# PSUM accumulators of a hybrid attention and recurrence layer: one pool of two banks, or a pool for each stage

## The chip, the cores and the metric

The kernel runs on one core of a Trainium2 chip. The metric is the device time of one execution in microseconds (us); the kernel before took 1431.96 us (median of three runs, 1424.61 to 1434.63). The engines are PE (TensorE, matrix products), DVE (VectorE), ACT (ScalarE), POOL (GpSimd) and SP (which issues the DMAs). A matrix product is written by PE into PSUM, a memory of eight banks, each of 512 fp32 numbers for each of 128 partitions, and is read from there by DVE or ACT, which is called its evacuation. A bank can take the next product only when its evacuation has ended.

## The reference

One decoder layer on 1024 tokens of width 1024, in fp32:

```
h   = rmsnorm(x);  p = h @ W_in          # q,k,v of 3 head groups, gates, recurrence inputs, merge gates
A   = dilated sliding-window attention   # 3 groups x 8 heads of 64, (window, dilation) = (128,1), (512,4), (2048,16),
                                         # merged per head by the softmax denominators
B   = RWKV-7 recurrence                  # 8 heads of 64
yA  = (A * silu(zA)) @ W_up_attn;  yB = (B * silu(zB)) @ W_up_rwkv
out = (sigmoid(ga) * yA + sigmoid(gb) * yB) @ W_out
x   = x + rmsnorm(out)
```

## The kernel before, in words

Every large product is made of three fp32r products: activations and weights are split in a high and a low part (`whi` by DVE or ACT, L135 and L137, `wlo` by POOL, L138), and hi x hi, lo x hi and hi x lo are summed in one PSUM bank, a tile named `acc`. A projection (`proj_steps`) has for each 128 columns of W_in two halves of 512 tokens, and each half is a group of 24 matmuls into one `acc` tile, which `evac` then reads.

The program has three stages.

- The recurrence, from the start to about 565 us of the span. Its order on PE is written out by hand (the tables PROLOGUE and LOOP), with projections filled in between. It uses all eight banks: two for `acc`, six in four pools of its own (`ps_ch`, `ps_y`, `ps_g`, `ps_i`).
- The attention, about 565 to 1155 us: four head pairs of about 150 us, each with three groups g = 0, 1, 2. For a group come the projections of q (evacuated by ACT L852 and DVE L853 for each of two heads), k (ACT L860, DVE L862), and v (DVE L888). The scores of a head are eight small products into tiles `pw` (L874, L875), each read at once by DVE (L876), which adds the bias and leaves a row maximum in `st`; `nm` (L879) is its negative, and ACT takes eight exponentials (L882). Tiles `pw` also take the transposes of v (L893, read by ACT L896 and DVE L897), of the weights (L949, read by ACT L952 as `ph` and DVE L953 as `pl`) and of `st` (L977). The products with v go to tiles `pv` (L961, L963), read into `num` by ACT L970 and DVE L971. After the third group of a pair, `group_weights` sends the maxima and sums through DRAM (tiles `mt`, `md`, `gs`; DVE L979, L980, then L998 to L1009).
- The last part, to the end: the remaining gate projections (evacuated by DVE L467), the two up-projections (L788 to L790, evacuated by DVE L1057 and L1073), and the product with W_out (L1102 to L1104), whose weights are loaded and split during the up-projection of the attention.

The pool `accp` of two banks (L224) is open for the whole program. In the attention `ps_w` (L804) has four banks and `ps_pv` two; in the last part only the two `acc` banks are used, and six stand empty. Beyond the recurrence the order of instructions on each engine is chosen by the framework's scheduler, which simulates a timeline and takes the instructions roughly in program order. The order is fixed before the program runs; an engine whose next instruction must wait holds up all that stand behind it.

Of the kernel before, what the change touches and what calls it, by code (L numbers as in the profile page):

```python
# [14 lines left out]
PSUM = bass.MemoryType.PSUM  # L15
# [97 lines left out]
class Kernel:  # L113
# [103 lines left out]
    def start(self):  # L217
        nc, tc, ctx, a = self.nc, self.tc, self.ctx, self.a
        pool = lambda **k: ctx.enter_context(tc.tile_pool(**k))
        self.cst = cst = pool(name="cst", bufs=1)  # L220
        self.wst = pool(name="wst", bufs=3)
        self.whl = pool(name="whl", bufs=3)
        self.ev = pool(name="ev", bufs=2)
        self.acc = pool(name="accp", bufs=2, space=PSUM)  # L224
        self.dram = pool(name="dram", bufs=1, space=DRAM)
        self.hstack = ExitStack()
        self.hpool = self.hstack.enter_context(tc.tile_pool(name="hT", bufs=1, side="right"))
        self.w_in = a["w_in"][0]
        self.sstack = ExitStack()
        self.small = self.sstack.enter_context(tc.tile_pool(name="small", bufs=1))  # L230

        self.ident = cst.tile([P, P], F32, name="ident")
        make_identity(nc, self.ident)
        self.eps = cst.tile([P, 3], F32, name="eps")
        nc.vector.memset(self.eps[:, 0:1], RMS_EPS)
        nc.vector.memset(self.eps[:, 1:2], GN_EPS)
        nc.vector.memset(self.eps[:, 2:3], 0.0)
        self.gain = cst.tile([P, KT], F32, name="gain")
        warm = cst.tile([P, 1], F32, name="warm")
        nc.scalar.activation(warm, self.eps[:, 2:3], AF.Sqrt)  # L240

        self.hT = []
        xr = a["x"][0].rearrange("(i r) d -> r i d", r=16)
        with tc.tile_pool(name="xin", bufs=1) as xin, tc.tile_pool(name="xps", bufs=4, space=PSUM) as xps:
            tiles = []

            def load(t):
                x = xin.tile([P, D], F32, name="x", tag="x", bufs=5)
                nc.sync.dma_start(x[0:64], xr[2 * t])
                nc.sync.dma_start(x[64:128], xr[2 * t + 1])  # L250
                tiles.append(x)

            for t in range(4):
                load(t)
            nc.sync.dma_start(self.gain, a["pre_norm_gain"].rearrange("o (k p) -> p (o k)", p=P))
            self.small_loads()
            for half in range(2):
                hh = self.hpool.tile([P, KT, 512], F32R, name=f"hh{half}")
                hl = self.hpool.tile([P, KT, 512], F32R, name=f"hl{half}")
                self.hT.append((hh, hl))  # L260
                if half:
                    self.w_wa = self.load_split(self.w_in, KT, OFF_WA)
                xs = []
                for j in range(4):
                    if half:
                        load(4 + j)
                    x = tiles[half * 4 + j]
                    sq = xin.tile([P, D], F32, name="sq", tag="sq", bufs=2)
                    st = xin.tile([P, 2], F32, name="st", tag="st", bufs=4)
                    if half:  # L270
                        nc.vector.tensor_tensor_reduce(sq, x, x, 1.0, 0.0, ALU.mult, ALU.add, st[:, 0:1])
                    else:
                        nc.scalar.activation(sq, x, AF.Square, accum_out=st[:, 0:1])
                    nc.scalar.activation(st[:, 1:2], st[:, 0:1], AF.Sqrt, bias=self.eps[:, 0:1], scale=1.0 / D)
                    nc.vector.reciprocal(st[:, 0:1], st[:, 1:2])
                    xn = xin.tile([P, D], F32, name="xn", tag="xn", bufs=5)
                    nc.vector.tensor_scalar(xn, x, st[:, 0:1], None, ALU.mult)
                    xs.append(xn)
                for k in range(KT):
                    ps = xps.tile([P, 512], F32, name="xT", tag="xT")  # L280
                    for j in range(4):
                        nc.tensor.transpose(ps[:, j * P:(j + 1) * P], xs[j][:, k * P:(k + 1) * P], self.ident)
                    nc.scalar.activation(hh[:, k], ps, AF.Copy, scale=self.gain[:, k:k + 1])
                    nc.vector.scalar_tensor_tensor(hl[:, k], ps, self.gain[:, k:k + 1], hh[:, k].bitcast(F32),
                                                   ALU.mult, ALU.subtract)
# [61 lines left out]
    def rwkv(self):  # L347
# [5 lines left out]
        with ExitStack() as ctx:  # L353
            pool = lambda **k: ctx.enter_context(tc.tile_pool(**k))
# [3 lines left out]
            self.ps_y = pool(name="ps_y", bufs=1, space=PSUM)  # L358
            self.ps_g = pool(name="ps_g", bufs=2, space=PSUM)
            self.ps_i = pool(name="ps_i", bufs=1, space=PSUM)  # L360

            self.sgn = rc.tile([P, 1], F32, name="sgn")
            nc.vector.memset(self.sgn[0:C], -1.0)
# [430 lines left out]
    def attention(self):  # L794
        nc, tc, a, cst = self.nc, self.tc, self.a, self.cst
        self.oat_d = self.dram.tile([NPAIR, P, S], F32, name="oat_d")
        self.n_md = 0
        self.hi_on_dve = True
        with ExitStack() as ctx:
            pool = lambda **k: ctx.enter_context(tc.tile_pool(**k))  # L800
            self.at = at = pool(name="at", bufs=1, side="right")
            early = ExitStack()
            self.ae = ae = early.enter_context(tc.tile_pool(name="ae", bufs=1))
            self.ps_w = pool(name="ps_w", bufs=4, space=PSUM)  # L804
            self.ps_pv = pool(name="ps_pv", bufs=2, space=PSUM)
            self.bias = []
            for i in range(2):
                b = ae.tile([P, 640], F32, name=f"bias{i}")
                nc.vector.memset(b[:, 512:], NEG)
                self.bias.append(b)  # L810

            self.kl = [ae.tile([P, S], F32R, name=f"kl{h}") for h in range(2)]
            for h in range(2):
                nc.vector.memset(self.kl[h][64 - 64 * h:128 - 64 * h].bitcast(F32), 0.0)
            for hp in range(NPAIR):
                self.attn_pair(hp)
            early.close()
            self.rwkv_parts()
# [212 lines left out]
    def finish(self):  # L1031
        nc, tc, a = self.nc, self.tc, self.a
        with ExitStack() as ctx:
            pool = lambda **k: ctx.enter_context(tc.tile_pool(**k))
            fin = pool(name="fin", bufs=1)
            quarter = lambda name: fin.tile([P, 512], F32, name=name, tag="gl", bufs=4)
            whole, orw = self.whole, self.orw
            for d in range(EARLY, KT):
# [123 lines left out]
```

## Time and profile before

| | |
|---|---|
| runs | 1424.61, 1431.96, 1434.63 us (median 1431.96) |
| profiled execution | 1427.3 us, span 1425.5 us, mean granted clock of TensorE 0.979 |
| PE busy | 1334.2 us, 94% of the span |
| DVE, ACT, POOL busy | 780.5, 575.4, 477.4 us |
| PE busy from 565 to 1155 us (attention) | 568.73 of 590.00 us |
| PE busy from 1155 to 1418 us (last part) | 247.67 of 263.00 us |

Times are from the start of the span. "Busy" of an engine counts the time in which one of its instructions runs. In the list of waits, "PE acc L142 <- DVE kl L862: 10.9, 6, 2.6" says that PE stood idle before matmuls of line 142 into a tile `acc` until DVE's instruction of line 862 had ended, 10.9 us in total, six times, the longest 2.6 us. In a timeline a row gives the start, the duration, engine, line and operation, output <- inputs, and in brackets the idle time before it with what ended it. PEclk is the granted clock of TensorE as a share of full speed.

### The profile page before, as it was taken

How to read it: one execution, taken by the hardware profiler on the slowest of the kernel's cores; microseconds unless marked ns; L12 is line 12 of the kernel's file. 1: busy time of each engine (PE TensorE's matmuls, PEld its weight loads, DVE VectorE, ACT ScalarE, POOL GpSimd, SP SyncE). 2: the span in 40 equal slices, each digit the busy share in tenths (PEclk: the TensorE clock that was granted, in tenths of full speed). 3: DMA queues.
4: the chain of work that ended last, by engine and by line, in shares of the span. 5: the costliest groups of instructions: out<-in, count | busy, mean ns of one | idle time of the engine just before them, and what ended most of it. 6: DMA issues, size and time to landing. Idle time of an engine off the chain costs nothing. (4 is left out here: it accounts for less than half of the span.)

```text
span 1425.5 us, 25770 instructions
## 1 busy us (share of the span) xinstructions
PE 1334.2 (94%) x10078; PEld 1118.8 (78%) x10078; DVE 780.5 (55%) x1675; ACT 575.4 (40%) x1378; POOL 477.4 (33%) x378
## 2 busy tenths in 40 slices
PE   4998799999999999999989998999899999998997
PEld 3898799777777777888868886888678877776886
DVE  5302755656565433465686558754776577338523
ACT  4435665654665332254426433543344320003211
POOL 1335534643453333322132223222223234434300
PEclk9998899999999999999999999999999999999999
DMA  8583444323332222111131112111221145654216
GB/s 170 156 241 103 119 103 120 98 71 80 106 80 57 77 77 86 46 35 52 36 96 46 41 47 75 54 50 37 58 74 31 40 150 176 201 168 141 73 35 172
DMA packets 199230, 131.17 MB, mean 92 GB/s; under 512 B 52788, under 2 KB 179340, under 8 KB 199108
## 3 DMA queue, kind: packets, MB, share of 16 engines
q1 hardware_dynamic: 199108, 129.52, 33.0%
q8 instruction: 79, 1.29, 0.4%
q14 instruction: 43, 0.35, 0.1%
HBM read 100.31 MB, written 33.89 MB: 94 GB/s over the span
## 5 line engine op out<-in xcount | busy, mean ns | idle before, releaser
L142 PE MATMUL acc<-hh,whi 128*128 128x512 f32 (+1 forms) x1360 | 480.0, 376 | 24.8 <-DVE kl L862 10.9
L142 PE MATMUL acc<-hh,wlo 128*128 128x512 f32 (+1 forms) x1360 | 469.8, 369 | 2.0 <-POOL wlo L138 1.9
L142 PE MATMUL acc<-hl,whi 128*128 128x512 f32 (+1 forms) x1360 | 469.8, 369 | 0.0
L138 POOL TENSOR_TENSOR wlo<-wstage,whi 128x512 fp32r<-128x512 f32 x186 | 250.8, 1349 | 532.2 <-DVE whi L135 262.2
L142 PEld LDWEIGHTS acc<-hh,whi 128*128 128x128 f32 x1360 | 247.7, 192 | 70.8 <-issue 16.9
L142 PEld LDWEIGHTS acc<-hh,wlo 128*128 128x128 f32 x1360 | 247.6, 192 | 41.1 <-POOL wlo L138 3.7
L142 PEld LDWEIGHTS acc<-hl,whi 128*128 128x128 f32 x1360 | 247.5, 192 | 35.3 <-issue 1.7
L882 ACT ACTIVATE L<-L,nm 128x128 f32<-128x128 f32 (+1 forms) x192 | 83.9, 438 | 84.6 <-DVE nm L879 84.4
L876 DVE CUSTOM_DVE_ANT_0 L<-pw,bias 128x128 f32<-128x128 f32 (+1 forms) x192 | 62.4, 350 | 51.6 <-PE pw L875 51.1
L861 POOL CAST k<-k 64x512 fp32r<-64x512 f32 x48 | 47.4, 988 | 107.0 <-ACT k L860 98.4
L135 DVE CAST whi<-wstage 128x512 fp32r<-128x512 f32 x108 | 53.2, 494 | 50.7 <-PE acc L142 32.3
L860 ACT CAST k<-acc 64x512 fp32r<-64x512 f32 x48 | 42.9, 894 | 75.4 <-DVE kl L862 51.9
L137 ACT CAST whi<-wstage 128x512 fp32r<-128x512 f32 x78 | 48.4, 621 | 61.0 <-PE acc L142 28.8
L852 ACT ACTIVATE q<-acc 64x512 fp32r<-64x512 f32 x48 | 43.9, 914 | 57.8 <-DVE q L853 28.6
L862 DVE TENSOR_TENSOR kl<-acc,k 64x512 fp32r<-64x512 f32 x48 | 45.7, 952 | 33.8 <-ACT k L860 33.4
L624 DVE TENSOR_TENSOR xtmp<-xinv 64x14 f32<-64x14 f32 (+6 forms) x112 | 33.5, 299 | 44.4 <-DMA xinv<-tin_d 41.5
L853 DVE SCALAR_TENSOR_TENSOR q<-acc,q 64x512 fp32r<-64x512 f32 x48 | 44.8, 933 | 20.9 <-ACT q L852 20.1
L952 ACT CAST ph<-pw 128x512 fp32r<-128x512 f32 x72 | 40.8, 583 | 36.0 <-PE pv L961 19.4
L953 DVE TENSOR_TENSOR pl<-pw,ph 128x512 fp32r<-128x512 f32 x72 | 47.2, 670 | 11.7 <-ACT ph L952 10.4
L875 PE MATMUL pw<-kl,q 128*128 128x128 f32 (+1 forms) x192 | 50.6, 278 | 1.4 <-DVE kl L862 1.4
L1102 PE MATMUL acc<-wo,mh 128*128 128x512 f32 x128 | 49.8, 389 | 0.0
L1103 PE MATMUL acc<-wo,mh 128*128 128x512 f32 x128 | 49.8, 389 | 0.0
(229 smaller groups left out, 2173.3 us busy)
## 6 DMA issues: line engine op xcount, KB each, us to landing
wstage<-in_w_in_dram SPq DMA_DIRECT2D x170, 256.0 KB
x<-in_x_dram SPq DMA_DIRECT2D x32, 256.0 KB
raw<-raw_d SPq DMA_DIRECT2D x24, 258.0 KB
raw_d<-rv SPq DMA_DIRECT2D x24, 256.0 KB
wb<-wd SPq DMA_DIRECT2D x24, 256.0 KB
bias_d<-bias_r SPq DMA_DIRECT2D x24, 192.0 KB
tb_d<-tb SPq DMA_DIRECT2D x16, 256.0 KB
ga_d<-tb SPq DMA_DIRECT2D x16, 256.0 KB
```

Of the source, the lines that this page charges most:

```text
L135: self.nc.vector.tensor_copy(hi, x)
L137: self.nc.scalar.copy(hi, x)
L138: self.nc.gpsimd.tensor_tensor(lo, x, hi.bitcast(F32), ALU.subtract)
L142: ins = self.nc.tensor.matmul(*args, **kw)
L861: nc.gpsimd.tensor_copy(self.gview(ks2[h][b], g, half), hi.bitcast(F32))
L862: nc.vector.tensor_tensor(self.gview(kl[h][a], g, half), pv, hi.bitcast(F32), ALU.subtract)
L875: nc.tensor.matmul(ps[:, :w], qs2[h][:, qc], kl[h][:, kc], start=False, stop=True)
L876: nc.vector.tensor_tensor_reduce(l[:, l0:l0 + w], ps[:, :w], self.bias[h][:, bo:bo + w], 1.0, -3.0e38, ALU.add, ALU.max, st[:, gi, 0, h, n ...
L882: nc.scalar.activation(ls, ls, AF.Exp, bias=nm[:, n:n + 1], scale=1.0, accum_out=st[:, gi, 1, h, n:n + 1])
L953: nc.vector.tensor_tensor(pl[:, :cw], ps[:, :cw], ph[:, :cw].bitcast(F32), ALU.subtract)
L1102: nc.tensor.matmul(ps, mh[k][:, ts], wh[:, k], start=k == 0, stop=False)
L1103: nc.tensor.matmul(ps, mh[k][:, ts], wl[:, k], start=False, stop=False)
```

## The change

The one pool of two accumulator banks is replaced by a pool for each stage: `accr` with two banks in the recurrence, `acca` with three in the attention, `accf` with four in the last part. `ps_w` in the attention goes from four banks to three. `ps_pv` stays at two.

```diff
-        self.acc = pool(name="accp", bufs=2, space=PSUM)          # start()
...
             self.ps_i = pool(name="ps_i", bufs=1, space=PSUM)
+            self.acc = pool(name="accr", bufs=2, space=PSUM)      # rwkv()
...
-            self.ps_w = pool(name="ps_w", bufs=4, space=PSUM)
+            self.acc = pool(name="acca", bufs=3, space=PSUM)      # attention()
+            self.ps_w = pool(name="ps_w", bufs=3, space=PSUM)
             self.ps_pv = pool(name="ps_pv", bufs=2, space=PSUM)
...
             fin = pool(name="fin", bufs=1)
+            self.acc = pool(name="accf", bufs=4, space=PSUM)      # finish()
```

Banks by the compiled programs: before, `accp` 0 and 1, `ps_w` 2 to 5, `ps_pv` 6 and 7. After, `accr` 6 and 7, `acca` 0 to 2, `ps_w` 3 to 5, `ps_pv` 6 and 7, `accf` 0 to 3. Since `accf` lies on `acca` and on a bank of `ps_w`, a tile of it comes after the tiles of the attention in those banks. Lines from 361 on stand one lower or higher in the changed file (L874 becomes L875, L876 becomes L877).

The order of PE is the same, row by row, through the recurrence; behind it the scheduler has chosen another one. Numbers in the names of tiles differ by a few between the two programs (`pw_7200` before is `pw_7204` after).

PE in the first head pair, end of the scores of group 0 (`pw_7200` to `pw_7212` are the last four of eight, then transposes of v and of the weights), before:

```order
L874 MATMUL pw_7200<-k1_6995,q1_6993 128x256
L875 MATMUL pw_7200<-kl1_6980,q1_6993 128x256
L142 MATMUL acc_7470<-hl1_212,whi_7437 128x512
L874 MATMUL pw_7204<-k1_6995,q1_6993 128x256
...
L875 MATMUL pw_7212<-kl1_6980,q1_6993 128x256
L142 MATMUL acc_7470<-hh1_211,wlo_7438 128x512
...
L893 MATMUL pw_7292<-ident_78,t4_7226 128x128 x4
L893 MATMUL pw_7299<-ident_78,t4_7226 128x128 x4
L949 MATMUL pw_7309<-ident_78,L0_7140 128x128 x4
L949 MATMUL pw_7322<-ident_78,L0_7140 128x128 x4
```

and now:

```order
L142 MATMUL acc_7515<-hh0_122,wlo_7512 128x512
L875 MATMUL pw_7204<-k1_6999,q1_6997 128x256
L876 MATMUL pw_7204<-kl1_6984,q1_6997 128x256
...
L876 MATMUL pw_7216<-kl1_6984,q1_6997 128x256
L894 MATMUL pw_7296<-ident_75,t4_7230 128x128 x4
L894 MATMUL pw_7303<-ident_75,t4_7230 128x128 x4
L950 MATMUL pw_7313<-ident_75,L0_7144 128x128 x4
L142 MATMUL acc_7546<-hh1_208,whi_7505 128x512
```

Seven matmuls of `acc_7470` stood between the last scores and the transposes; now seven tiles `pw` follow one another.

DVE at the same place, before:

```order
L853 SCALAR_TENSOR_TENSOR q0_7425<-acc_7441,q0_7425 64x2x256
L135 CAST whi_7507<-wstage_7505 128x512
L876 ISA L1_7183,st_6991<-pw_7200,bias1_6977 128x256
...
L876 ISA L1_7183,st_6991<-pw_7204,bias1_6977 128x256
...
L876 ISA L1_7183,st_6991<-pw_7208,bias1_6977 128x256
...
L876 ISA L1_7183,st_6991<-pw_7212,bias1_6977 128x256
...
L853 SCALAR_TENSOR_TENSOR q1_7426<-acc_7441,q1_7426 64x2x256
```

and now:

```order
L854 SCALAR_TENSOR_TENSOR q0_7429<-acc_7474,q0_7429 64x2x256
L877 ISA L1_7187,st_6995<-pw_7204,bias1_6981 128x256
...
L877 ISA L1_7187,st_6995<-pw_7208,bias1_6981 128x256
...
L863 TENSOR_TENSOR kl0_6983<-acc_7515,k0_7431 64x2x256
L877 ISA L1_7187,st_6995<-pw_7212,bias1_6981 128x256
...
L877 ISA L1_7187,st_6995<-pw_7216,bias1_6981 128x256
...
L854 SCALAR_TENSOR_TENSOR q1_7430<-acc_7445,q1_7430 64x2x256
```

An evacuation of k (`kl0`) now stands between the reads of the last four scores.

PE at the end of the attention (fourth pair; `pw_12191` is the transpose of `st`, `acc_12533` the first gate projection), before:

```order
L977 MATMUL pw_12191<-ident_78,st_11110 96x128
L893 MATMUL pw_12291<-ident_78,t4_12225 128x128 x4
L893 MATMUL pw_12298<-ident_78,t4_12225 128x128 x4
L949 MATMUL pw_12308<-ident_78,L0_12105 128x128 x4
L142 MATMUL acc_12425<-hh1_211,wlo_12396 128x512
L142 MATMUL acc_12533<-hh0_125,whi_12523 128x512
...
L949 MATMUL pw_12325<-ident_78,L0_12105 128x128 x4
```

and now:

```order
L978 MATMUL pw_12195<-ident_75,st_11114 96x128
L894 MATMUL pw_12295<-ident_75,t4_12229 128x128 x4
L894 MATMUL pw_12302<-ident_75,t4_12229 128x128 x4
L950 MATMUL pw_12312<-ident_75,L0_12109 128x128 x4
L950 MATMUL pw_12329<-ident_75,L0_12109 128x128 x4
L950 MATMUL pw_12352<-ident_75,L1_12152 128x128 x4
L962 MATMUL pv_12310<-ph_12317,v_12294 128x128
...
L964 MATMUL pv_12350<-pl_12358,v_12294 64x128
L142 MATMUL acc_12541<-hh0_122,whi_12531 128x512
```

Before, the gate projection stands in the middle of the last transposes and products; now it (`acc_12541`) comes after all but the last products with v. The last projection of the attention, `acc_12429`, ends before the last seven scores.

DVE at that place now:

```order
L954 TENSOR_TENSOR pl_12335<-pw_12329,ph_12334 128x512
L999 TENSOR_TENSOR gm_12212<-gs_12202 8x256
L1000 TENSOR_TENSOR gm_12212<-gm_12212,gs_12202 8x256
L954 TENSOR_TENSOR pl_12358<-pw_12352,ph_12357 128x512
L1002 TENSOR_TENSOR gs_12202<-gs_12202,gm_12212 8x4x64 x2
L1002 TENSOR_TENSOR gs_12202<-gs_12202,gm_12212 8x256
L972 TENSOR_TENSOR num_12309<-num_12309,pv_12310 64x512
```

`pl_12358` and the read of `pv_12310` stand behind instructions on `gs`, which a DMA brings.

## Rows read from the trace of the kernel before

**Rows 1.** Waits of PE, 565 to 1155 us (total, times, longest)

```profile
PE acc L142 <- DVE kl L862: 10.9, 6, 2.6
PE acc L142 <- DVE q L853: 6.5, 6, 2.5
```

**Rows 2.** Waits of PE, 1155 us to the end

```profile
PE acc L142 <- DVE tb L467: 6.3, 4, 2.8
PE acc L788 <- DVE gl L1073: 4.3, 5, 2.6
PE acc L788 <- DVE ml L1057: 3.6, 3, 2.1
```

**Rows 3.** Timeline of PE, two matmuls of one accumulator wait

```profile
725.02 0.39 PE L142 MATMUL acc<-hh,wlo 128*128 128x512 f32 x1
727.73 0.47 PE L142 MATMUL acc<-hh,whi 128*128 128x512 f32 x1 [2.32 <-DVE kl L862]
```

**Rows 4.** Stretches: length, busy PE, PEld, DVE, ACT, POOL; then PEclk, DMA share, GB/s

```profile
565.00:1155.00 590.00, 568.73 (x3026) 479.40 (x3025) 365.81 (x828) 251.36 (x626) 156.39 (x128) 0.99 0.18 51
569.00:574.00 5.00, 5.00 (x16) 3.96 (x16) 1.79 (x2) 1.05 (x1) 0.69 (x1) 0.66 0.36 105
1276.00:1280.00 4.00, 4.00 (x12) 3.12 (x11) 0.12 (x1) 0.23 (x1) 1.30 (x2) 0.57 0.61 189
109.00:120.00 11.00, 7.48 (x37) 7.42 (x38) 2.32 (x6) 8.64 (x23) 6.60 (x6) 0.53 0.16 50
1152.00:1169.00 17.00, 17.00 (x97) 14.39 (x97) 15.06 (x21) 4.24 (x7) 5.95 (x2) 1.00 0.63 204
```

**Rows 5.** Timeline of DVE, 604 to 612 us

```profile
605.85 0.42 DVE L876 CUSTOM_DVE_ANT_0 L<-pw,bias 128x256 f32<-128x256 f32 x1
606.76 1.09 DVE L853 SCALAR_TENSOR_TENSOR q<-acc,q 64x512 fp32r<-64x512 f32 x1 [0.48 <-ACT q L852]
```

**Rows 6.** Timeline of PE, 604 to 612 us

```profile
604.72 0.28 PE L874 MATMUL pw<-k,q 128*128 128x256 f32 x1
...
604.95 0.28 PE L874 MATMUL pw<-k,q 128*128 128x256 f32 x1
...
607.07 1.04 PE L893 MATMUL pw<-ident,t 128*128 128x128 f32 x8
607.95 1.04 PE L949 MATMUL pw<-ident,L 128*128 128x128 f32 x8
```

**Rows 7.** Instructions of line 860, 565 us on (count: shortest/median/longest ns, first, last)

```profile
L860 ACT CAST k<-acc x48: 580/1013/1185, 576.2 to 1122.9; 64x512 fp32r<-64x512 f32 x48
```

**Rows 8.** Timeline of DVE, end of the attention

```profile
1140.25 0.29 DVE L876 CUSTOM_DVE_ANT_0 L<-pw,bias 128x128 f32<-128x128 f32 x1
...
1140.59 0.17 DVE L879 TENSOR_SCALAR nm<-st 128x8 f32<-128x8 f32 x1
...
1149.20 0.29 DVE L980 COPY mt<-pw 32x128 f32<-32x128 f32 x1
...
1153.72 0.60 DVE L998 TENSOR_TENSOR gm<-gs 8x256 f32<-8x256 f32 x1 [1.56 <-DMA gs<-md]
1154.36 0.41 DVE L999 TENSOR_TENSOR gm<-gm,gs 8x256 f32<-8x256 f32 x1
1154.81 1.46 DVE L1001 TENSOR_TENSOR gs<-gs,gm 8x256 f32<-8x256 f32 x3
...
1158.65 0.67 DVE L971 TENSOR_TENSOR num<-num,pv 64x512 f32<-64x512 f32 x1
```

**Rows 9.** Timeline of ACT, the eighth exponential of that head

```profile
1143.51 0.39 ACT L882 ACTIVATE L<-L,nm 128x128 f32<-128x128 f32 x1
```

**Rows 10.** Timeline of DVE, up-projection of the attention begins

```profile
1274.16 0.43 DVE L135 CAST wo<-wstage 128x512 fp32r<-128x512 f32 x1 [5.37 <-DMA wstage<-in_w_out_dram]
```

**Rows 11.** Timeline of PE, one product pair of the attention

```profile
703.33 0.27 PE L961 MATMUL pv<-ph,v 128*128 128x128 f32 x1
...
703.50 0.27 PE L961 MATMUL pv<-ph,v 128*128 128x128 f32 x1
```

## The prediction

> **What bounds the kernel now.** I read the shares of busy time first: PE is at work 94% of the span, so it can gain only what it loses in idle time and at a low clock. Next I read PE's waits, stage by stage. In the attention PE stands idle 21.3 of 590 us [rows 4]; 17.4 of them are matmuls into a fresh `acc` tile that wait for DVE to finish reading k (10.9) or q (6.5) out of that bank [rows 1]. In the last part it is 6.3 behind the gates, 4.3 and 3.6 behind the two up-projections, 14.2 in all [rows 2]. So 31.6 us are waits for one of two banks. The timeline shows how one looks: the last matmul of a group starts at 725.02, the next one is let go by DVE and starts at 727.73, 2.32 us of idleness [rows 3]. Last I read the granted clock. Right behind a wait of 2 us or more stands a stretch at a reduced clock: seven such, the first from 569 to 574 at 0.66, the last from 1276 to 1280 at 0.57 [rows 4]. In these the time lost is 5.0 x 0.34 = 1.7 and 4.0 x 0.43 = 1.7 us; seven make 11.9 us, at the level of 1.2 instead of 2.4 GHz.
>
> **The recurrence** keeps two banks and its order on PE: nothing.
>
> **Attention, what is taken away.** A third bank lets a group of matmuls begin while two older ones are still being read. The 17.4 us of accumulator waits go. The rest of the 21.3 us of idleness (3.9) are waits for scores and products, which are contained in what follows; I take the whole 21.3 as removed and count every wait of the new order afresh.
>
> **Attention, what is added.** One score bank fewer, and an order that packs the `pw` tiles together. Take the end of the scores of group 0 in the first pair. PE now issues four scores, two transposes of v and one of the weights one behind the other. A pair of score matmuls takes 0.23 us and four transposes 0.44 [rows 6], so PE needs 4 x 0.23 + 3 x 0.44 = 2.2 us. With three banks each tile has to wait for the read of the third one before it. DVE reads a score in 0.42 [rows 5], but the evacuation `kl0` stands after the second; like q's it takes 1.09 [rows 5], and it needs ACT's copy of k first, 1.01 [rows 7], which begins when `acc_7515` is complete, 0.2 before the scores by the pitch. So `kl0` runs from 1.2 to 2.3, the last two scores to 3.1, and the transposes behind them end at 3.7. PE loses 3.7 - 2.2 = 1.5 us; when ACT still has a share of q ahead of it (one more instruction of 1.0), 2.5. Before, seven matmuls of `acc_7470` filled this place, and four banks took all four scores without a wait. I find this bunching at the ends of groups 0 and 1 in all four pairs, thus eight places; the second ones have five scores and three transposes, and the same sum gives 2.0 to 2.7. I take 2.5 x 8 = 20.0, and 0.5 for each of the first three ends of group 2, 1.5. Together 21.5 us. Ends: half of it, 10.8, if ACT is never ahead and the copies of weights hide one wait in two; double, 43, if DVE's next evacuations (two of q at 1.09, one of k) come before the reads of v, with the next transposes behind them.
>
> **The passage to the last part.** Now PE is busy 17.00 of 17.00 us there [rows 4], because gate projections fill the gaps in the last head's chain. In the new order none can: `acca`'s last projection is over before seven scores of that head, and the first `accf` tile comes after the eight matmuls into `pv_12350`. The chain, from there: seven scores read by DVE one at a time, 7 x 0.30 = 2.1 (128 wide, 0.29 [rows 8]); the negated maximum 0.17; eight exponentials, from 1140.76 when it ends to 1143.90 [rows 8, 9], 3.1; transpose and two copies 0.8; from the end of the second copy, 1149.49, to 1153.72 the trip through DRAM, 4.2 [rows 8]. DVE has `pl_12358` and the read of `pv_12310` behind that: 0.60 + 0.41, 0.67 for `pl`, 1.46, 0.67 [rows 8]. Then four product pairs at 0.17 [rows 11], 0.7, and 1.0 for five hand-overs of some 0.2 each. Sum 15.9. PE has in it 7 x 0.17 (scores of 128), five batches of transposes (2.2) and twelve product pairs (2.0), 5.4 us. Idle: **10.5 us**. Ends: 4, if PE is late there by some of its other waits and the exponentials end before it arrives; 14, if the DRAM trip is longer.
>
> **Last part.** Four banks: a group now waits for a bank that was filled four groups earlier, about 22 us at 5.5 us a group. The 14.2 us go. But some of these waits were caused by DVE being late as a whole. At 1274.16 DVE has waited 5.37 us for the weights of W_out, and the weights of the next group (`whi`) stand behind that wait [rows 10]; DVE is busy 15.06 of 17 us from 1152 on [rows 4]. With the bank free PE would stop for `whi` and `wlo` instead. I leave 4 of the 14.2: -10.2. Ends: -14.2 and -4.
>
> **Clock.** The seven stretches go (-11.9), since their waits do. Of the new waits about four reach 2.5 us, 4 x 1.7 = +6.8. The passage's gaps are longer; behind longer waits early in the program stands a stretch of 11 us at 0.53, 5.2 us lost [rows 4]. I take 4.2. Together -0.9; from -8 (no new stretch in the attention) to +6 (eight).
>
> A rule of the skill speaks on what the third bank can give: the Trainium skill, "Perfetto Trace Analysis", section "Matmul Optimizations", wants all eight PSUM banks used. Here the attention uses eight before and after, so by the rule it gains nothing; only the last part would, which goes from two to four. That alone would be a gain of 14.2 plus three stretches of clock.
>
> **Sum:** -21.3 + 21.5 + 10.5 - 10.2 - 0.9 = -0.4, on the profiled execution's 1427.3: 1426.9. That execution lies 4.7 below the median of the runs shown, 1431.96. Against the median: about **1431**. No change beyond 1% (14.3 us), which is what a measurement of this kernel can tell.
>
> **The rivals.**
>
> *Bunching hidden, faster (0.22).* PE gets ahead of DVE by a further bank, so that at the eight places half or less is lost, because the scheduler has put the scores where DVE is free (DVE is busy 366 of 590 us [rows 4], 62%). Against it: DVE's reads at these places are in the order itself, `kl0` in the middle. Attention 10.8 instead of 21.5, clock 4 less, passage 6 instead of 10.5: -19.6. About 1412.
>
> *All bank waits vanish with nothing in their place (0.08).* The 31.6 us go, and 11.9 of clock: -43.5. About 1388. For it speaks that the waits repeat at the same lines; against it the order above, and that four `ps_w` banks were in use. The Trainium skill says just this in "Perfetto Trace Analysis", section "Optimization Strategy": the same gap repeating on the engine that should be saturated can mean too little PSUM for the next tile. The trace agrees that the gap is a bank's (rows of k and q), but no row shows what the bank taken from the scores costs.
>
> *Three score banks bind, slower (0.26).* The mechanism is DVE's order at the eight places: an evacuation of q or k between the reads of scores holds a score bank, and with it PE. If two such evacuations (2 x 1.09) stand between the reads instead of one, or if each is itself late for ACT's copy, a place costs 4.5 to 5, and nearly every place is followed by a stretch of low clock. Attention +38 for 21.5, clock +5 more: +21, about 1453. It decides from 4.3 us a place (14.3 / 8 more than 2.5).
>
> That the change does not do what it says can be left at nothing: the bank numbers of the compiled program show it.
>
> **Chances.** Forecast (within 1%) 0.44; hidden 0.22 and all gone 0.08, of which some of the former lies within 1%; slower 0.26. Faster by over 1% 0.29, within 1% 0.45, slower by over 1% 0.26. The range goes from 1407 (half the bunching, a shorter passage and a full gain in the last part, without the all-gone case) to 1453 (the third rival); a tenth lies out on each side. The forecast's own range is 1419 to 1444.
>
> **What would show it.** In the changed kernel's waits: no more `acc <- kl` and `acc <- q` rows, and in their place `pw <- L` (DVE's read of scores, line 877), `pw <- v` and `pw <- ph` rows of some 20 us over the attention. In the timeline: a gap of PE of about 10 us, in pieces, before the first gate projection of the last part, against none now. In the last part: waits for `whi` and `wlo` of about 4 us, none for `tb`, `ml`, `gl`. In the clock: stretches at half rate behind the new gaps, not at the old places. I am wrong if the waits for `pw` are under 10 us (faster) or over 35 (slower), or if the scheduler's passage costs nothing since PE arrives late there.

## The result: 0.65% slower

The changed kernel took 1436.43 us (median of 14 runs, 1433.19 to 1442.17), the kernel before 1425.37 in the 14 runs beside it; ratio 1.0065, 95% interval 1.0049 to 1.0081. Its profiled execution took 1434.99 us, 7.7 more than the one before (1427.3). Forecast was no change: 1431, with 1427 for a profiled execution.

The page's first part (busy time, share of the span, instructions) shows the same work on PE spread over a longer span:

```profile
PE 1338.8 (93%) x10078; PEld 1120.7 (78%) x10078; DVE 780.4 (54%) x1675; ACT 577.1 (40%) x1378; POOL 476.1 (33%) x378
```

Waits of PE in the changed kernel from 565 to 1155 us, which answer to [rows 1] (total, times, longest; line 875 is the first matmul of a score, 877 its read by DVE, 894 the transposes of v):

```profile
PE pw L875 <- DVE st L877: 17.3, 18, 1.7
PE acc L142 <- DVE q L854: 4.5, 7, 1.4
PE pw L894 <- DVE st L877: 3.2, 2, 2.3
PE pv L962 <- DVE num L972: 0.6, 2, 0.3
```

The waits for k are gone, those for q have fallen from 6.5 to 4.5, and 20.5 us of waits for a score bank have come. The same view from 1155 us on answers to [rows 2]:

```profile
PE pw L978 <- ACT L L883: 3.8, 1, 3.8
PE acc L142 <- DVE whi L135: 3.3, 1, 3.3
PE pv L962 <- DVE num L972: 2.4, 1, 2.4
PE acc L788 <- DVE gl L1075: 1.5, 4, 0.6
PE acc L1104 <- ACT mh L1077: 1.2, 1, 1.2
PE acc L142 <- POOL wlo L138: 1.0, 1, 1.0
```

The first and third are the passage, in which PE did not wait before (1152 to 1169 in [rows 4]). The gates' waits (6.3) are gone, and 4.3 us of waits for weights stand there. Stretches (length, busy PE, PEld, DVE, ACT, POOL, then PEclk, DMA share, GB/s), which answer to [rows 4]:

```profile
565.00:1155.00 590.00, 563.41 (x2974) 471.13 (x2973) 359.46 (x810) 245.75 (x606) 155.69 (x128) 0.99 0.18 50
760.00:765.00 5.00, 4.18 (x18) 3.33 (x19) 3.34 (x10) 3.67 (x15) 0.00 (x0) 0.66 0.50 167
1035.00:1045.00 10.00, 8.90 (x44) 7.31 (x44) 4.99 (x14) 1.16 (x2) 1.28 (x1) 0.83 0.36 81
1065.00:1075.00 10.00, 7.66 (x33) 6.12 (x32) 9.72 (x21) 6.72 (x13) 4.27 (x3) 0.83 0.27 92
1155.00:1175.00 20.00, 13.74 (x67) 12.08 (x67) 14.38 (x31) 9.42 (x28) 0.00 (x0) 0.66 0.37 125
1210.00:1220.00 10.00, 6.71 (x18) 5.04 (x18) 8.55 (x11) 1.27 (x2) 2.55 (x2) 0.66 0.36 125
```

Attention: 26.6 us of idleness against 21.3. Passage (1155 to 1175): 6.3 idle, and 20 x 0.34 = 6.8 of lost clock, where before PE was busy without a gap at full clock. The lost clock from 565 us on is 1.7 + 1.7 + 1.7 + 6.8 + 3.4 = 15.3 against 11.9. This counts low clock also where PE stood idle and lost nothing by it. Weighted with PE's busy time, in slices of 1 us, the loss is about 13.2 (5.5 of it in the passage) against 11.9.

One place shows what a score waits for. In DVE's and PE's timelines near 746 us, in the second head pair (L917 and L918 are two instructions of the merge of the first pair, L916 and L917 before):

```profile
742.76 1.98 DVE L917 TENSOR_TENSOR wb<-num,wb 128x1024 f32<-128x1024 f32 x1 [1.49 <-DMA wb<-wd]
744.78 1.23 DVE L918 TENSOR_TENSOR t<-t,wb 128x1024 f32<-128x1024 f32 x1
745.92 0.42 DVE L877 CUSTOM_DVE_ANT_0 L<-pw,bias 128x256 f32<-128x256 f32 x1
```

```profile
746.40 0.39 PE L875 MATMUL pw<-k,q 128*128 128x256 f32 x1 [1.68 <-DVE st L877]
760.46 1.09 PE L894 MATMUL pw<-ident,t 128*128 128x128 f32 x8 [2.27 <-DVE st L877]
```

The read of a score at 745.92 stands behind 3.2 us of merge on DVE, and PE waits 1.68 us for its bank. Pairs two to four have such waits between about 730 and 760, 883 and 914, 1036 and 1069; the first pair, which has no merge ahead of it, loses 0.9 us. The longest one, 2.27 us before 760.46, stands behind evacuations of q and the last part of the merge (L923, L924).

The bracket of the first row shows that the merge costs DVE more than its length: DVE had stood 1.49 us for the tile `wb`, which a DMA brings, and all that is queued behind stood too. DVE's waits for `wb` from 565 to 1155 us, first before, then in the changed kernel:

```profile
DVE t L911 <- DMA wb<-wd: 6.8, 3, 2.4
DVE wb L916 <- DMA wb<-wd: 1.5, 3, 0.7
```

```profile
DVE t L912 <- DMA wb<-wd: 12.9, 3, 5.0
DVE wb L917 <- DMA wb<-wd: 12.4, 4, 4.0
```

### The profile page after: what moved, and what is told of

Its sections match the earlier page's. It is cut to its first block, busy times and chain, and to the rows that moved or that the text cites. A ratio compares the mean times of both kernels' runs of the same rounds, so it can differ in the third digit from the quotient of the medians.

```text
span 1433.1 us, 25735 instructions
## 1 busy us (share of the span) xinstructions
PE 1338.8 (93%) x10078; PEld 1120.7 (78%) x10078; DVE 780.4 (54%) x1675; ACT 577.1 (40%) x1378; POOL 476.1 (33%) x378
## 5 line engine op out<-in xcount | busy, mean ns | idle before, releaser
L877 DVE CUSTOM_DVE_ANT_0 L<-pw,bias 128x128 f32<-128x128 f32 (+1 forms) x192 | 63.0, 348 | 72.6 <-PE pw L876 71.7
L135 DVE CAST whi<-wstage 128x512 fp32r<-128x512 f32 x108 | 53.7, 498 | 70.3 <-issue 32.3
L875 PE MATMUL pw<-k,q 128*128 128x128 f32 (+1 forms) x192 | 52.0, 284 | 17.7 <-DVE st L877 17.3
L971 ACT COPY num<-pv 64x512 f32<-64x512 f32 x48 | 27.2, 584 | 82.1 <-PE pv L964 81.6
L875 PEld LDWEIGHTS pw<-k,q 128*128 128x128 f32 x192 | 36.3, 189 | 29.3 <-DVE st L877 24.6
L854 DVE SCALAR_TENSOR_TENSOR q<-acc,q 64x512 fp32r<-64x512 f32 x48 | 43.9, 930 | 18.3 <-ACT q L853 17.4
L863 DVE TENSOR_TENSOR kl<-acc,k 64x512 fp32r<-64x512 f32 x48 | 46.1, 961 | 10.5 <-ACT k L861 9.5
```

The costliest lines, as they stand in the source:

```text
L135: self.nc.vector.tensor_copy(hi, x)
L854: nc.vector.scalar_tensor_tensor(self.gview(qs2[h][b], g, half), pv, 0.125, hi.bitcast(F32), ALU.mult, ALU.subtract)
L863: nc.vector.tensor_tensor(self.gview(kl[h][a], g, half), pv, hi.bitcast(F32), ALU.subtract)
L875: nc.tensor.matmul(ps[:, :w], qs2[h][:, qc], ks2[h][:, kc], start=True, stop=False)
L877: nc.vector.tensor_tensor_reduce(l[:, l0:l0 + w], ps[:, :w], self.bias[h][:, bo:bo + w], 1.0, -3.0e38, ALU.add, ALU.max, st[:, gi, 0, h, n ...
```

## The experiments

All were timed in five rounds beside the kernel before, with four (pw3) to twelve executions each. The scheduler chooses the order of instructions anew for each program, so an edit can change more than it says; where the traces show the same order in two programs, or another one, this is said. "q to up" is the time in a profile from DVE's first evacuation of q to the first matmul of the up-projections; it is 664.8 us before (565.5 to 1230.3) and 682.4 after (563.7 to 1246.1). "Up to end" runs from there to the start of PE's last matmul: 186.3 before, 178.1 after.

| kernel | acc, score banks in attention | acc in the last part | ratio to before (95%) | q to up | up to end |
|---|---|---|---|---|---|
| changed | 3, 3 | 4 from its start | 1.0065 (1.0049 to 1.0081) | 682.4 | 178.1 |
| fin4_early | 2, 4 | 4 from its start | 0.9965 (0.9943 to 0.9986) | 666.5 | 181.1 |
| fin4_late | 2, 4 | 2, then 4 from up on | 0.9958 (0.9935 to 0.9981) | 663.3 | 180.6 |
| fin4_mid | 2, 4 | 2, then 4 from the second gate on | 0.9952 (0.9929 to 0.9974) | 661.2 | 180.7 |
| att3_keep | 3, 3 | the same 3 | 0.9994 (0.9972 to 1.0016) | 669.4 | 180.5 |
| att3_fin4_late | 3, 3 | 3, then 4 from up on | 0.9995 (0.9975 to 1.0015) | 671.1 | 179.0 |
| pw3 | 2, 3 | the same 2 | 1.0130 (1.0112 to 1.0148) | 680.2 | 184.4 |
| pw3_early | 2, 3 | 4 from its start | 1.0134 (1.0101 to 1.0167) | 687.4 | 177.7 |

**fin4_late** takes the last part alone, behind the gates:

```diff
+            self.acc = pool(name="accf", bufs=4, space=PSUM)   # behind the gate loop in finish()
             self.hstack.close()
```

> The kernel before with its two accumulator banks and four score banks, and a pool of four accumulator banks opened behind the gate projections, for the two up-projections and the product with W_out only. Theory (the changed kernel gains 10.2 us between the first matmul of the up-projections and that of W_out, 99.5 before against 89.3, because the bank waits there go; it loses more than that at the passage from the attention to the last part): the gain stays without the loss, about 10 us below the kernel before, 1415. Rival (the loss is the third score bank's, in the attention): also 1415, this run does not tell the two apart. If the up-projections are paced by the splitting of the weights, whatever the banks: no gain, 1425.

Measured 0.9958, about 6 us faster, not 10: up to end fell by 5.7. Waits for the up-projections' evacuation:

```profile
PE acc L142 <- DVE tb L467: 6.2, 4, 3.0
PE acc L788 <- DVE gl L1074: 3.7, 6, 1.2
```

Those for `ml` are gone, some for `gl` stay with four banks. The gates, with two, wait as before. By operation and tile, the order of instructions on PE, DVE, ACT and POOL is that of the kernel before throughout, so the gain is the banks' alone.

**att3_keep** keeps `acca` open to the end:

```diff
-            self.acc = pool(name="acca", bufs=3, space=PSUM)   # inside the attention's pools
+        self.acc = self.ctx.enter_context(tc.tile_pool(name="acca", bufs=3, space=PSUM))   # ahead of them
...
-            self.acc = pool(name="accf", bufs=4, space=PSUM)
```

> Three accumulator and three score banks in the attention as in the change, but the three accumulator banks stay open to the end, so that gate projections can again stand between the last transposes and products of the attention. Theory (passage): no gap of PE before the first gate projection of the last part, against 6.3 us of waits and 6.9 us of lost clock between 1155 and 1175 in the changed kernel; attention about 3 dearer than before, up-projections 6 to 10 cheaper: 1417 to 1423, below the kernel before. Rival (score banks): 20.5 us of waits behind score reads stay in the attention and the time stays at 1430 to 1436.

> As the run before it (three accumulator banks kept through the passage, three score banks), with four further accumulator banks from the up-projections on. Theory: 0 to 4 us below that run, since a third bank already takes most of the waits of the up-projections; 1415 to 1421. Rival (score banks): 1430.

The second run keeps these three banks through the gates and opens `accf` behind them. Both land on the kernel before (0.9994 and 0.9995), between the theory and its rival. The two programs have the same order on all engines; the fourth bank behind the gates brings nothing measurable. The passage is closed, as this stretch of att3_keep shows:

```profile
1155.00:1175.00 20.00, 20.00 (x96) 16.77 (x95) 7.36 (x25) 6.39 (x32) 5.08 (x4) 1.00 0.27 79
```

Against the changed kernel, whose attention has the same banks and, up to 1153 us, the same order on PE, that is worth 0.7%, 10 us. But the score waits stay in the attention:

```profile
PE pw L875 <- DVE st L877: 15.3, 16, 1.9
PE acc L142 <- DVE q L854: 4.3, 6, 1.4
PE pw L894 <- DVE st L877: 3.2, 2, 2.2
```

**fin4_early** gives the changed kernel its old attention:

```diff
-            self.acc = pool(name="acca", bufs=3, space=PSUM)
-            self.ps_w = pool(name="ps_w", bufs=3, space=PSUM)
+            self.acc = pool(name="acca", bufs=2, space=PSUM)
+            self.ps_w = pool(name="ps_w", bufs=4, space=PSUM)
```

> The change with two accumulator and four score banks in the attention, as before; the four accumulator banks of the last part are opened at its start, on banks of the attention, as in the change. Theory (passage): the gap of PE before the first gate projection comes as in the changed kernel, about 13 us with the clock, against some 10 to 12 gained in the last part: 1425 to 1432, while attention's waits are those of before (k and q, about 17 us). Rival (score banks): without the lost score bank nothing is lost, 1412 to 1416.

It is faster than before, 0.9965, and not separable from fin4_late: opening `accf` early is nearly free here, so the theory as I had it fell. The stretches of its passage (columns as above) have 3.0 us of idleness and 3.4 of lost clock:

```profile
1140.00:1155.00 15.00, 13.71 (x86) 11.73 (x84) 6.56 (x18) 6.63 (x23) 2.56 (x2) 1.00 0.16 42
1155.00:1175.00 20.00, 18.28 (x77) 15.25 (x78) 19.84 (x25) 3.06 (x5) 5.63 (x3) 0.83 0.61 212
```

Where the cover comes from is seen in the ranges of two lines, the evacuation of z (L904) and the reads of scores (L877): first fin4_early, then the changed kernel (count, shortest/median/longest ns, first and last start).

```profile
L904 DVE COPY t<-acc x8: 679/686/692, 693.7 to 1150.9; 128x512 f32<-128x512 f32 x8
L877 DVE CUSTOM_DVE_ANT_0 L<-pw,bias x192: 263/293/432, 592.2 to 1140.9; 128x128 f32<-128x128 f32 x104, 128x256 f32<-128x256 f32 x88
```

```profile
L904 DVE COPY t<-acc x8: 684/689/694, 684.5 to 1153.5; 128x512 f32<-128x512 f32 x8
L877 DVE CUSTOM_DVE_ANT_0 L<-pw,bias x192: 270/293/426, 585.5 to 1155.7; 128x128 f32<-128x128 f32 x104, 128x256 f32<-128x256 f32 x88
```

With four score banks the last scores are read 10 us before the last projection (z) ends, which so covers the exponentials; with three they come 2 us behind it, and nothing is left to cover them once the gates are shut out.

**pw3** and **pw3_early** take one score bank and give no accumulator for it:

```diff
-            self.ps_w = pool(name="ps_w", bufs=4, space=PSUM)   # pw3: the kernel before
+            self.ps_w = pool(name="ps_w", bufs=3, space=PSUM)
...
-            self.acc = pool(name="acca", bufs=3, space=PSUM)    # pw3_early: the changed kernel
+            self.acc = pool(name="acca", bufs=2, space=PSUM)
```

> The kernel before with three score banks instead of four and nothing else; a bank stands empty. Theory A (the loss in the attention is the score bank's, the third accumulator gives something back): accumulator waits of 17 us stay and score waits of 15 to 20 us come on top; 15 to 20 us above before, 1440 to 1446. Theory B (both kinds of wait are DVE being late, and a wait at one place only moves the other): the sum of PE's waits in the attention stays at 20 to 26 us, score waits take the place of some accumulator waits; 0 to 6 us above before, 1425 to 1435.

> The changed kernel with two accumulator banks in the attention instead of three (three score banks, four accumulator banks from the start of the last part). Theory A (the uncovered passage comes from the third accumulator, which lets the last projection run ahead of the last scores): the passage is as cheap as with two and four banks, about 2 us, and the time is that of three score banks alone minus 6 in the last part. Theory B (it comes from the three score banks, which put the last scores behind the last projection): the waits between 1150 and 1175 are as in the changed kernel, about 6 us and as much of lost clock, and the time is 1432 to 1440.

pw3 loses 1.3%, about 18 us: theory A's size. From 590 us on its order on PE is another one, so this is the price of a score bank with the order that the scheduler makes for three. Its waits, 560 to 1150 us:

```profile
PE pw L874 <- DVE st L876: 15.6, 14, 2.0
PE pw L893 <- DVE st L876: 4.5, 8, 0.9
PE acc L142 <- DVE kl L862: 4.5, 5, 1.2
PE acc L142 <- DVE q L853: 3.0, 2, 2.5
```

Not by the sum I gave for it: 20.1 us of score waits came, and of 17.4 us of accumulator waits 7.5 stayed, not all. The idleness of PE accounts for 9.1 of its 15.4 us in "q to up" (36.7 against 27.5); the other 6.3 are longer busy time for the same matmuls, of which low clock explains about 2. Its profile is also 4.4 us longer ahead of the attention, where the edit changes nothing; this stays open. The third accumulator, att3_keep against pw3, gives back 1.4%, 10.8 us of it in "q to up" and 3.9 in the last part. So the trade of banks in the attention is, in "q to up", a loss of 15.4 us against a gain of 10.8. pw3_early has the gap at the passage with two accumulators too: theory B, three score banks make it (4.8 us behind the exponentials, 2.8 behind `num`; in fin4_early the first is gone, and 2.4 behind `num` stay). Its time, 1444.78, is above the 1432 to 1440 I gave for that theory; pw3, without that gap, already took 1446.52.

**after_vact** and **fin4_late_vact** move one evacuation from DVE to ACT:

```diff
-                      lambda half, ps: nc.vector.tensor_copy(self.gview(vt, g, half), self.pview(ps, g)))
+                      lambda half, ps: nc.scalar.copy(self.gview(vt, g, half), self.pview(ps, g)))
```

> The changed kernel with the evacuation of the v projections moved from DVE to ACT (24 instructions of 1.04 us). If DVE's lateness in the attention sets the waits for scores: the 20.5 us of score waits fall by 5 or more and the time by as much, 1425 to 1431. If ACT's share of q and k, which DVE waits for, is the limit, the waits grow and the time with them: 1436 to 1442.

> The run fin4_late (two accumulator and four score banks, four accumulator banks from the up-projections on) with the evacuation of the v projections moved from DVE to ACT. If DVE's lateness sets the accumulator waits of the attention: its 17 us of waits fall by 5 or more and the time lies 5 to 10 below fin4_late, 1411 to 1416. If ACT is the limit: 1421 or more.

Neither moves: 1.0081 (1.0060 to 1.0102) beside 1.0065, 0.9947 (0.9933 to 0.9961) beside 0.9958. DVE's total load is not what the score banks wait for: 25 us less of it left 15.8 + 3.2 of 20.5 us of score waits.

**after_mergepool** and **fin4_late_mergepool** take the long instructions out of DVE's queue:

```diff
-                nc.vector.tensor_tensor(r3(o), nums[g].rearrange("p (i r) -> p r i", r=16), r3(w), ALU.mult)
+                nc.gpsimd.tensor_tensor(r3(o), nums[g].rearrange("p (i r) -> p r i", r=16), r3(w), ALU.mult)
...
-            nc.vector.tensor_tensor(w4, n, w4, ALU.mult)
-            nc.vector.tensor_tensor(o, o, w, ALU.add)
+            nc.gpsimd.tensor_tensor(w4, n, w4, ALU.mult)
+            nc.gpsimd.tensor_tensor(o, o, w, ALU.add)
```

> The changed kernel with the first part of the merge of a head pair (L912, L917, L918: five instructions of 1.2 to 2.0 us a pair) moved from DVE to POOL. In its trace these stand on DVE between the reads of scores of the next pair, and 18 of the 20.5 us of score waits lie in the 45 us in which they run. Theory (a long DVE instruction between the reads holds three score banks): score waits fall to 10 us or less, the time by 8 to 12, to 1424 to 1429. Rival (the waits come from the evacuations of q and k that also stand there): score waits stay above 16 and the time at 1434 to 1438. If POOL then delivers wlo too late, waits for wlo appear.

> The same move of the merge to POOL in the run fin4_late (two accumulator, four score banks). Its 15.6 us of accumulator waits lie in part in the same stretches behind the merge: 3 to 8 us below fin4_late if DVE's merge sets them, equal if the chain from PE over ACT to DVE of one bank does.

Waits of after_mergepool, 560 to 1150 us:

```profile
PE acc L142 <- DVE q L854: 10.2, 3, 8.3
PE pv L964 <- DVE pl L954: 2.8, 4, 1.0
PE pw L950 <- DVE v L898: 2.7, 1, 2.7
PE acc L142 <- POOL wlo L138: 2.6, 2, 1.3
PE pw L875 <- DVE st L877: 1.9, 3, 0.8
PE pw L894 <- DVE st L877: 0.9, 1, 0.9
```

The score waits fall from 20.5 to 2.8 us, so with this part of the merge out of DVE's queue they go. Two things go with it: DVE's waits for `wb`, and the order of PE, which is another one from 737 us on. The run therefore does not tell the length of the merge from the DMA wait ahead of it, nor either from the new order. PE's idleness from 565 to 1155 us falls only from 26.6 to 23.5 us, and the time to 1.0031 (1.0008 to 1.0055): other waits come, the longest because the merge takes longer on POOL and ACT's next step, `tz`, stands ahead of its share of q. ACT's timeline around that one wait of 8.3 us:

```profile
916.16 0.63 ACT L922 ACTIVATE tz<-t 128x512 f32<-128x512 f32 x1 [13.77 <-POOL t L918]
916.82 1.97 ACT L853 ACTIVATE q<-acc 64x512 fp32r<-64x512 f32 x2
```

With four score banks the move gains nothing measurable (0.9953, 0.9926 to 0.9980). Yet the merge matters there too. In fin4_late (first row) the merge is on DVE; with the move (the other two) the waits for k are gone, and waits for score banks and for q have taken their place:

```profile
PE acc L142 <- DVE kl L862: 11.2, 6, 2.7
```

```profile
PE pw L893 <- DVE st L876: 10.3, 4, 4.0
PE acc L142 <- DVE q L853: 10.2, 8, 2.5
```

So four score banks can run out as well, in another order of PE and with this part of the merge off DVE.

**fin4_mid** opens the four banks one gate later than fin4_early and five gates earlier than fin4_late:

```diff
+            accf = pool(name="accf", bufs=4, space=PSUM)
             for d in range(EARLY, KT):
+                if d == EARLY + 1:
+                    self.acc = accf
```

> The kernel before with four more accumulator banks from the second of the six gate projections on, so that the first gate still covers the end of the attention. fin4_late has 6.2 us of waits for the gates' evacuation and 3.5 us of lost clock behind them. If banks set these: 4 to 8 below fin4_late, 1413 to 1417. If DVE's splitting of the weights, which stands in the same queue, is late then: a wait for whi or wlo takes their place and the time is that of fin4_late within 3 us.

0.9952, the same as fin4_late. The waits for `tb` are gone, and 4.3 us for `wlo` and `whi` have come for 6.2: the gates are paced by their weights.

**att3_fin4_late_mergepool** joins the closed passage with the merge on POOL.

> att3_fin4_late (three accumulator and three score banks, passage covered by gate projections, four accumulator banks from the up-projections on) with the merge on POOL as in after_mergepool. If the merge on DVE is what makes three score banks dear: score waits fall from 20.8 us to under 8, and with the passage covered the time is 5 to 12 below the kernel before, as good as fin4_late or better, 1412 to 1420. If the slower merge on POOL gives the gain back by a wait of q (8.3 us in after_mergepool): 1420 to 1426.

0.9982 (0.9956 to 1.0008): score waits 2.8 us as expected, but the wait for q is there again (8.1 us). No arrangement with three score banks had a ratio below those of the versions with four, though this last one (up to 1.0008, from 0.9956) is not clear of them. Of those with four, fin4_late, fin4_mid and fin4_early are 0.4 to 0.5% faster than the kernel before and, dividing the ratios, about 1% faster than the changed one.

## Why the prediction was wrong

The forecast was no change, as the sum of large terms of both signs. The change made the kernel 0.65% slower, about 9 us, clear of an interval of 0.16% to either side; the 1% that I took for the limit of a measurement was too wide. The terms, by the two profiles:

| term | forecast | measured |
|---|---|---|
| attention, idleness | -21.3 + 21.5 = +0.2 | 26.6 - 21.3 = +5.3 |
| passage, idleness | +10.5 | +6.3 |
| last part, waits | -10.2 | 7.0 - 14.2 = -7.2 |
| clock | -0.9 | 15.3 - 11.9 = +3.4 |
| sum | -0.4 | +7.8 |

The sum lies near the 7.7 between the profiled executions by luck. From the first evacuation of q to the last matmul the changed kernel is 9.4 us longer (860.5 against 851.1), and ahead of that, where the order on PE is the same, its profile is 1.8 shorter. Of the 9.4, 4.2 are idleness and 5.2 longer busy time of PE for the same 4096 matmuls. Low clock, weighted with busy time, makes about 1.3 of the 5.2, not 3.4; no run shows what makes the rest.

- **"The 17.4 us of accumulator waits go"** is the step that failed first. 4.5 us for q stayed with three banks, all of it new idleness against the forecast. The count of score waits, 21.5, was nearly what came (20.5), but by luck, for a reason that was wrong: I had put them at eight ends of groups behind an evacuation of k. The first of these places cost 1.3 us (0.9 for a score bank, 0.5 for q), not 2.5; about 19 of the 20.5 us stand in the three stretches in which the merge of the pair before runs on DVE, and in after_mergepool they go with it. I had read the order at group ends and not asked which long instructions, and which waits for a DMA, share DVE's queue with the reads.
- **Clock.** I let seven stretches go and four plus a passage come back. In the attention three remained instead of four (5.1 us), but the passage lost 6.8, not 4.2, and a wait of 3.3 us for `whi` in the gates brought 3.4, which I had not priced: I had left 4 us of waits for weights there and no clock behind them. (Weighted with busy time, the passage lost 5.5 and the gates 2.9.) My reading that low clock stands right behind each wait of 2 us or more fits only in part: before, the wait of 2.63 us that ends at 1291.02 has full clock behind it (1.00 from 1288 to 1300), and in the changed kernel the stretch from 1038 on stands behind waits of 0.68 and 0.30 us.
- **Passage.** The chain was right: exponentials, transpose, DRAM, `pl`, `num`, then the gates. From the end of the last projection to the first gate projection it took 16.6 us (1153.3 to 1169.9) against 15.9, but PE was busy in 9.8 of them, not in 5.4, in part because it worked at the low clock. So its idleness was dearer on paper (10.5 for 6.3); idleness and clock together are 13.1 (11.8 with the clock weighted) against 14.7. The DRAM trip left no wait of its own: DVE read v and `pl` meanwhile. That three score banks are needed for it, and not only a pool opened late, I had not seen; fin4_early and pw3_early show it.
- **Last part.** The bank waits went as forecast; 7.0 us stayed or came for 4. The third rival ("three score banks bind") had the right sign, and DVE's queue as the place, but evacuations of q and k as the cause.
- The rule of "Perfetto Trace Analysis" in the Trainium skill, section "Matmul Optimizations" (use all eight banks), agrees with the runs for the one stage that used two of eight: it gains from more (0.9958). On dividing eight banks anew, by which the attention lost, the section says nothing.

Shown by experiment: that more banks in the last part gain 6 us, that closing the passage is worth 10 us with three score banks, and that, when `accf` is opened early, three score banks make the wait for the exponentials, the longest at the passage. Shown only together with a new order of PE: the price of the score bank, what the third accumulator gives back, and that the score waits go when the merge leaves DVE's queue. Not shown: whether the merge's length or its wait for `wb` makes them. Only read from the order and the traces: that the last z projection covers the tail in fin4_early.

## What to carry to other kernels

When banks are moved from one pool to another, look for the longest hold-up in the queue that reads them, an instruction together with what it waits for: a pool must bridge it, and short products need more banks for it than long ones (a score is made in 0.23 us, an accumulator in 5.5). A pool that opens on another stage's banks shuts out the work that used to cover that stage's tail, so keep a few banks open across the seam and widen behind it. Where the last of several stages leaves banks empty, widen only there.

## What the runs showed of the hardware

DVE's cast of 128x512 weights (L135) took 0.43 us in the median, and in the attention of the changed kernel at most 1.3. With the merge on POOL it took up to 2.6 us: two of them 4.82 together from 900.47, beside POOL's L917 (899.53, 2.93 us) and L918 (902.54, 2.46 us). The Trainium skill, "SBUF — State Buffer", section "Who interferes with whom", says that DVE in a two-port mode and GpSimd take a shared port in turn, each for its whole instruction; the durations agree, though no run here shows in which mode the cast ran. From 565 to 1155 us some 80 casts took 46 us in all instead of 35, so work moved from DVE to POOL (22.9 us on DVE) was in part paid by DVE.
